# The diagonal of a gated scan: wide products by a matrix of ones, or sixteen one-column fp32 products

## The chip, the core and the metric

The kernel runs on one core of a Trainium2 chip. The metric is the device time of one execution in microseconds (us), as the median of several runs; the kernel before takes 483.58 us (three runs, 483.41 to 483.65). Engines are named as in the profile: PE is the matrix engine (TensorE), PEld its weight loads, DVE the vector engine, ACT the scalar engine, POOL GpSimd, SP the engine that issues most DMAs.

## What is computed

The reference is one decoder layer on 256 tokens of width 1024. A normalised input goes through one wide projection `w_in`. Its columns feed two branches: HGRN2, a gated linear recurrence with 8 heads of 128 channels, and block attention with 8 heads of 128. Both are projected, gated, summed, projected again, and a SwiGLU feed-forward part follows. All arrays are fp32.

The change touches the recurrence alone. Inside a chunk the reference computes

```
diff  = b[:, :, :, None, :] - b[:, :, None, :, :]
decay = exp(where(causal, diff, -inf))
attn  = einsum('bhtk,bhsk,bhtsk->bhts', q_, k_, decay)
```

where `b` is the running sum of the log gates. On the diagonal, t equals s, the decay is 1, and the entry is the plain sum over the 128 channels k of q times k at that token. That diagonal, for 2 blocks of 128 tokens and 8 heads, is what the changed code produces.

## The kernel before, in words

**Layout.** Tokens are handled in two blocks of 128. For the recurrence, `Q`, `K` and the gate `Fg` lie with channels on the partitions: [128 channels, 2 token blocks, 8 heads, 128 tokens]. The scores `A` of the recurrence lie as [128 tokens, 2 blocks, 8 heads, 128 tokens]. A routine `hgrn_diag` writes the diagonal (and zeros beside it) into all of `A`; then seven levels, `hgrn_level(0)` to `hgrn_level(6)`, lay the off-diagonal squares of doubling size over it with `COPY_PREDICATED` (L383). So `A` has to hold the diagonal before level 0 copies into it.

**Precision.** PE multiplies the big projections in the type fp32r. To keep fp32 precision each operand is cut in two halves, a high one (a cast on ACT, L55) and a low one (a subtraction on DVE, L56), and each product is made of three matmuls: high by high, high by low, low by high. Weights arrive by DMA as `wraw` and become `whi` and `wlo`; each of the three names has three buffers. `tok_block` (L83, L84, L85) is such a projection with 8 chunks of 128 rows by 512 columns for two token blocks: 48 matmuls, on two loads of weights of 4 chunks each. A matmul whose operands are plain fp32 needs no halves; the trace then shows two weight loads and two matmul records for one instruction.

**The diagonal before.** `hgrn_diag` multiplies Q by K into `qk` on DVE (L346), casts the high half `qkh` on ACT and subtracts the low half `qkl` on DVE (helper `split`, L55 and L56). `hgrn_diag_put` then runs, for two token blocks and two groups of four heads, two matmuls with a 128 x 128 matrix of ones as stationary operand and 512 columns of a half as moving operand (L356): each output row holds the sum over channels. DVE multiplies the result by the identity into `A` (L357), four times.

**Around it.** PE has just finished the two halves of the attention keys (`ktok`, columns 5120 and up). After the diagonal come level 0 (16 fp32 matmuls of 64 x 64, L377, on half the array's columns each), the first half of the attention queries (`qtok`, 48 wide matmuls), level 1, and the transposes of `ktok` (L422). Before those, `keys` normalises `ktok`: sums of squares on ACT (L413), scale and square root and reciprocal (L216, L217, L218), and two multiplications on DVE (L432).

**Order.** Up to the end of the attention a scheduler orders each engine's instructions when the program is built; each engine then runs its own list in order and waits on semaphores. PE takes the weights of the next matmul while one runs. From the middle stage on, the order is written out by hand and is the same in both kernels.

Of the kernel before, what the change touches and what calls it, by code (L numbers as in the profile page):

```python
# [7 lines left out]
F32 = mybir.dt.float32  # L8
F32R = mybir.dt.float32r
# [5 lines left out]
P = 128  # L15
# [3 lines left out]
H = 8  # L19
# [8 lines left out]
def tile_hgrn2_moba_block(ctx: ExitStack, tc: tile.TileContext, xm, xw, table, runs,  # L28
                          w_in, w_hg, w_at, w_out, w_gate, w_up, w_down, out):
    nc = tc.nc  # L30
    const = ctx.enter_context(tc.tile_pool(name="const", bufs=1))
    big = ctx.enter_context(tc.tile_pool(name="big", bufs=1))
    wp = ctx.enter_context(tc.tile_pool(name="wp", bufs=3))
    small = ctx.enter_context(tc.tile_pool(name="small", bufs=1))
# [9 lines left out]
    def pa(name="pa"):  # L44
        return psum.tile([P, 512], F32, name=name, tag="pa", bufs=2)
# [8 lines left out]
    def split(src, hi, lo):  # L54
        high = nc.scalar.copy(hi, src)  # L55
        return high, nc.vector.tensor_sub(lo, src, hi.bitcast(F32))  # L56
# [79 lines left out]
    for kt in range(KT):  # L136
        n0 = 0 if kt == 0 else NV
        t = big.tile([P, NX + D - n0], F32, name=f"xw{kt}", tag=("T3", "T4", "T5", "T1", "T7", "T8", "T9", "T11")[kt])
# [8 lines left out]
    ones = const.tile([P, P], F32, name="ones")  # L147
# [47 lines left out]
    ones_r = const.tile([P, P], F32R, name="ones_r")  # L195
    nc.gpsimd.tensor_copy(ones_r, ones)
    ident = const.tile([P, P], F32, name="ident")
# [6 lines left out]
    for j in range(7):  # L204
        c = 1 << j
        n = 64 // c
        for tb in range(2):
            m = mask[:, j, tb, :].rearrange("p (n c) -> p n c", c=c)
# [70 lines left out]
    for half in range(2):  # L279
        ps = F0 if half == 0 else feat_block(w_in, 1024 + half * 512, XT, cut=2 - half)  # L280
        for j in range(2):
            h = half * 4 + j * 2
# [44 lines left out]
    for half in range(2):  # L327
        ps = feat_block(w_in, half * 512, XT)
        for j in range(2):
            h = half * 4 + j * 2  # L330
# [7 lines left out]
    A = big.tile([P, 2, H, P], F32, name="A", tag="T5")  # L338
# [2 lines left out]

    def hgrn_diag():
        qk = big.tile([P, 2, H, P], F32, name="qk", tag="T9")
        qkh = big.tile([P, 2, H, P], F32R, name="qkh", tag="T10")
        qkl = big.tile([P, 2, H, P], F32R, name="qkl", tag="T8")
        nc.vector.tensor_mul(qk, Q, K)  # L346
        nc.vector.tensor_mul(QA, Q, Fg)
        split(qk, qkh, qkl)
        return qkh, qkl

    def hgrn_diag_put(qkh, qkl):
        for tb in range(2):
            for g in range(2):
                bank = (ph, pa)[g]().rearrange("p (h t) -> p h t", h=4)
                for m, part in enumerate((qkh, qkl)):
                    nc.tensor.matmul(bank, ones_r, part[:, tb, 4 * g:4 * g + 4, :], start=(m == 0), stop=(m == 1))  # L356
                nc.vector.tensor_mul(A[:, tb, 4 * g:4 * g + 4, :], bank,  # L357
                                     ident.unsqueeze(1).to_broadcast([P, 4, P]))

    def hgrn_level(j, small_bank=ph):  # L360
        Fc = decay[j]
# [46 lines left out]
    def qk_block(tok, sq, c0, half, bank=pw):  # L408
        put_tok(tok, tok_block(w_in, c0 + half * 512, XT, bank=bank), half)
        for tb in range(2):  # L410
            for h in range(half * 4, half * 4 + 4):
                jk = small.tile([P, P], F32, name="jk")
                nc.scalar.activation(jk, tok[:, tb, h * P:(h + 1) * P], AF.Square, accum_out=sq[:, tb, h:h + 1])  # L413
# [89 lines left out]
    kss = small.tile([P, 2, H], F32, name="kss")  # L503
    qk_block(ktok, kss, 5120, 0, bank=pa)
    qk_block(ktok, kss, 5120, 1)
    qkd = hgrn_diag()
    hgrn_diag_put(*qkd)
    hgrn_level(0)
    qtok = big.tile([P, 2, D], F32, name="qtok", tag="T8")
    qss = small.tile([P, 2, H], F32, name="qss")  # L510
# [704 lines left out]
```

## Time and profile before

| | before |
|---|---|
| median of 3 runs | 483.58 us |
| the profiled execution | 483.81 us |
| its span, first to last instruction | 482.1 us |
| granted PE clock, mean over the span | 1.000 |
| PE busy | 477.1 us (99%) |
| DVE busy | 405.8 us (84%) |
| ACT busy | 322.2 us (67%) |
| POOL busy | 37.3 us (8%) |

The 1.7 us between the profiled execution's time and its span lie before its first and after its last instruction. A row of the timeline gives the start, the length, the engine, the line, the operation, output and inputs, the number of merged instructions, and in brackets how long the engine sat idle before it and what ended that. Matmul records overlap, since the next one starts streaming while the last one drains: the cost of a matmul in a row of them is the distance from start to start, not its length. Starts and ends are given to 0.01 us.

### The profile page before, as it was taken

The numbers are of one execution on the slowest core, as the hardware profiler recorded it, in microseconds if no ns is written. First come the engines' busy times: TensorE is split into PE (matmuls) and PEld (weight loads), VectorE is DVE, ScalarE is ACT, GpSimd is POOL, SyncE is SP. The second block draws the span as 40 slices with busy tenths as digits, with TensorE's granted clock in tenths as the row PEclk, the third lists the DMA queues.
The fourth block names the chain that finished last, engine by engine and source line by source line (L and its number), as shares of the span: only waits on it lengthen the run. The fifth ranks groups of instructions, "written<-read, shape, count | busy, mean of one in ns | idle before, by whom it ended". The sixth has DMA issues, their size and how long they took to land.

```text
span 482.1 us, 6427 instructions
## 1 busy us (share of the span) xinstructions
PE 477.1 (99%) x2514; PEld 399.5 (83%) x2514; DVE 405.8 (84%) x402; ACT 322.2 (67%) x433; POOL 37.3 (8%) x73
## 2 busy tenths in 40 slices
PE   8999999999999999999999999999999999999997
PEld 7888888888888889887888888888888888888886
DVE  5878999698669987989999667899999999788863
ACT  5978645768756985789767645776786559747520
POOL 0930220000000000010000000000000000000000
PEclk9999999999999999999999999999999999999999
DMA  8978595634542345978896764799978979996502
GB/s 295 402 263 257 152 334 176 208 109 126 198 147 69 128 154 183 388 217 235 255 277 193 232 209 170 247 281 230 333 261 218 337 196 283 365 253 136 175 0 87
DMA packets 44125, 105.83 MB, mean 220 GB/s; under 512 B 1848, under 2 KB 4152, under 8 KB 42304
## 3 DMA queue, kind: packets, MB, share of 16 engines
q1 hardware_dynamic: 41344, 88.11, 52.6%
q0 software_dynamic: 2752, 17.33, 17.1%
q8 instruction: 19, 0.31, 0.3%
q14 instruction: 10, 0.08, 0.0%
HBM read 89.67 MB, written 1.07 MB: 188 GB/s over the span
## 4 chain that ended last, share of the span: by engine, by line
PE 92%; DVE 4%; ACT 2%; DMA 1%; issue 0%; SPq 0%; ACTq 0%
PE acc L1065 12%; PE late L571 12%; PE pw L814 10%; PE f L571 6%; PE pw L101 6%; PE pw L83 5%; PE pw L84 5%; PE pw L85 5%; PE pw L960 5%; PE pw L165 4%; PE pa L571 3%; DVE wlo L552 2%; PE pw L100 2%; PE pw L103 2%; DMA xw<-xw 1%; PE pw L959 1%
## 5 line engine op out<-in xcount | busy, mean ns | idle before, releaser
L548 ACT CAST whi<-W 128x2048 fp32r<-128x2048 f32 x42 | 79.9, 1912 | 42.4 <-DVE W L639 23.4
L552 DVE TENSOR_TENSOR wlo<-W,whi 128x2048 fp32r<-128x2048 f32 x42 | 95.6, 2288 | 10.6 <-ACT whi L548 9.9
L552 DVE TENSOR_TENSOR wlo<-wraw,whi 128x2048 fp32r<-128x2048 f32 x29 | 66.2, 2288 | 7.5 <-ACT whi L548 7.3
L548 ACT CAST whi<-wraw 128x2048 fp32r<-128x2048 f32 x29 | 55.5, 1918 | 14.3 <-PE pw L814 7.0
L56 DVE TENSOR_TENSOR wlo<-wraw,whi 128x2048 fp32r<-128x2048 f32 (+1 forms) x26 | 55.0, 2125 | 10.8 <-ACT whi L55 10.7
L55 ACT CAST whi<-wraw 128x2048 fp32r<-128x2048 f32 (+1 forms) x26 | 46.0, 1779 | 10.3 <-PE pw L85 5.6
L83 PE MATMUL pw<-whi,XT 128*128 128x512 f32 x112 | 44.2, 395 | 0.0
L85 PE MATMUL pw<-whi,XT 128*128 128x512 f32 x112 | 43.8, 391 | 0.0
L84 PE MATMUL pw<-wlo,XT 128*128 128x512 f32 x112 | 43.7, 390 | 0.0
L101 PE MATMUL pw<-XT,whi 128*128 128x512 f32 x128 | 40.6, 395 | 0.0
L645 POOL DMA_DIRECT2D W<-W x14 | 12.1, 862 | 345.4 <-ACT whi L548 161.9
L960 PE MATMUL pw<-x2T,whi 128*128 128x512 f32 x96 | 31.2, 396 | 0.0
L571 PE MATMUL late<-whi,C 128*128 128x512 f32 x96 | 30.4, 392 | 0.0
L1065 PE MATMUL acc<-whi,hq 128*128 128x512 f32 x92 | 29.4, 393 | 0.0
L83 PEld LDWEIGHTS pw<-whi,XT 128*128 128x128 f32 x112 | 21.0, 188 | 4.4
L85 PEld LDWEIGHTS pw<-whi,XT 128*128 128x128 f32 x112 | 21.0, 188 | 4.3
L84 PEld LDWEIGHTS pw<-wlo,XT 128*128 128x128 f32 x112 | 21.1, 188 | 4.2
L571 PE MATMUL late<-whi,x2T 128*128 128x512 f32 x72 | 23.3, 394 | 0.0
L639 DVE TENSOR_TENSOR W<-W,W 128x2048 f32<-128x2048 f32 x10 | 22.9, 2288 | 0.2
L571 PEld LDWEIGHTS late<-whi,C 128*128 128x128 f32 x96 | 18.0, 188 | 3.9 <-ACT q L663 0.2
L571 PE MATMUL f<-whi,C 128*128 128x512 f32 x64 | 20.8, 396 | 0.2 <-ACT q L663 0.2
L814 PE MATMUL pw<-whi,M 128*128 128x512 f32 x64 | 20.7, 396 | 0.0
(339 smaller groups left out, 1117.9 us busy)
## 6 DMA issues: line engine op xcount, KB each, us to landing
wraw<-w_in SPq DMA_DIRECT2D x22, 1024.0 KB, 5.1
W<-W POOLq DMA_DIRECT2D x14, 1024.0 KB, 8.6
wraw<-w_down SPq DMA_DIRECT2D x11, 1024.0 KB, 7.8
W<-w_in SPq DMA_DIRECT2D x8, 1024.0 KB, 7.4
W<-w_gate SPq DMA_DIRECT2D x8, 1024.0 KB, 7.3
W<-w_up SPq DMA_DIRECT2D x8, 1024.0 KB, 8.5
wraw<-w_at SPq DMA_DIRECT2D x4, 1024.0 KB, 6.5
wraw<-w_hg SPq DMA_DIRECT2D x4, 1024.0 KB, 7.2
```

Source lines behind the costliest of these rows:

```text
L55: high = nc.scalar.copy(hi, src)
L56: return high, nc.vector.tensor_sub(lo, src, hi.bitcast(F32))
L83: nc.tensor.matmul(ps[tb], part(act, kt, 0)[:, ts], wh, start=(kt == 0), stop=False)
L84: nc.tensor.matmul(ps[tb], part(act, kt, 0)[:, ts], wl, start=False, stop=False)
L85: nc.tensor.matmul(ps[tb], part(act, kt, 1)[:, ts], wh, start=False, stop=(kt == KT - 1))
L101: nc.tensor.matmul(ps[ct], hi[:, i, cs], both, start=(kt == 0), stop=(kt == KT - 1))
L548: nc.scalar.copy(t["hi"], raw())
L552: nc.vector.tensor_sub(t["lo"], raw(), t["hi"].bitcast(F32))
L571: nc.tensor.matmul(bank, act(kt, m), h[:, kt, :], start=(first and kt == 0 and m == 0 and h is hi), stop=(kt == 3 and m == 1), skip_group_ ...
L814: nc.tensor.matmul(blocks[key][tb], part(act, k0 + i, m)[:, tb * P:(tb + 1) * P], t[w][:, i, :], start=(k0 + i == 0 and m == 0 and w == "hi"),
L960: nc.tensor.matmul(block["ps", up][ct], t["hi"][:, i, cs], both, start=(kt == 0), stop=(kt == KT - 1))
L1065: nc.tensor.matmul(bank, ACTS[f0 + i](m, ts), w[:, i, c0:c0 + cw], start=(st and i == 0 and m == 0 and w is t["hi"]), stop=(en and i == 1 ...
```

## The change

The halves `qkh` and `qkl` go, and with them a cast on ACT and a subtraction on DVE. The eight wide matmuls go. In their place 16 fp32 matmuls, one for each block and head, take a 128 x 128 piece of `qk` as the stationary operand and one column of ones as the moving operand; each writes one column of 128 tokens into one bank of PSUM. ACT copies the 16 columns to SBUF (`dd`). DVE multiplies the identity by `dd`, both repeated by stride 0, into `A`: two instructions of 1024 columns in place of four of 512. `Q` times `K` and `Q` times `Fg` stay.

```diff
     def hgrn_diag():
         qk = big.tile([P, 2, H, P], F32, name="qk", tag="T9")
-        qkh = big.tile([P, 2, H, P], F32R, name="qkh", tag="T10")
-        qkl = big.tile([P, 2, H, P], F32R, name="qkl", tag="T8")
         nc.vector.tensor_mul(qk, Q, K)
         nc.vector.tensor_mul(QA, Q, Fg)
-        split(qk, qkh, qkl)
-        return qkh, qkl
-
-    def hgrn_diag_put(qkh, qkl):
+        return qk
+
+    def hgrn_diag_put(qk):
+        bank = pa("diag")
         for tb in range(2):
-            for g in range(2):
-                bank = (ph, pa)[g]().rearrange("p (h t) -> p h t", h=4)
-                for m, part in enumerate((qkh, qkl)):
-                    nc.tensor.matmul(bank, ones_r, part[:, tb, 4 * g:4 * g + 4, :], start=(m == 0), stop=(m == 1))
-                nc.vector.tensor_mul(A[:, tb, 4 * g:4 * g + 4, :], bank,
-                                     ident.unsqueeze(1).to_broadcast([P, 4, P]))
+            for h in range(H):
+                c = tb * H + h
+                nc.tensor.matmul(bank[:, c:c + 1], qk[:, tb, h, :], ones[:, 0:1], start=True, stop=True)
+        dd = small.tile([P, 2, H], F32, name="dd")
+        nc.scalar.copy(dd.rearrange("p b h -> p (b h)"), bank[:, 0:2 * H])
+        for tb in range(2):
+            nc.vector.tensor_mul(A[:, tb], ident.unsqueeze(1).to_broadcast([P, H, P]),
+                                 dd[:, tb, :].unsqueeze(2).to_broadcast([P, H, P]))
...
-    qkd = hgrn_diag()
-    hgrn_diag_put(*qkd)
+    hgrn_diag_put(hgrn_diag())
```

The scheduler also moves neighbours. On ACT, around the end of `ktok` and the normalisation of the keys (a row gives line, operation, output and inputs, shape, and how often it stands in a row; + is new, - is gone):

```order
 L259 ACTIVATE ktok<-pw,rx 128x512
 L413 ACTIVATE jk,kss<-ktok 128x128
+L355 COPY dd<-diag 128x16
 L55 CAST whi<-wraw 128x2048
 L413 ACTIVATE jk,kss<-ktok 128x128
 L365 COPY KP<-K 128x2x256x2
 L413 ACTIVATE jk,kss<-ktok 128x128 x5
+L55 CAST whi<-wraw 128x2048
 L217 ACT_TABLE_LOAD
 L217 ACTIVATE rk<-rk 128x16
-L55 CAST whi<-wraw 128x2048
```

The copy of `dd` stands ahead of a weight cast, the remaining sums of squares and the copy `KP`; the next weight cast moved ahead of the square root `rk`.

On DVE, before, from level 0's copies into `A` to level 1's (`rk` is the scale of the keys, `wlo` the low half of a weight chunk):

```order
L383 COPY_PREDICATED A<-mask,ph 64x8x32 x4
L394 TENSOR_TENSOR QA<-QA,Fg 128x2x512
L396 TENSOR_TENSOR K<-K,F_976 128x2x256x2
L216 TENSOR_SCALAR rk<-kss 128x16
L56 TENSOR_TENSOR wlo<-wraw,whi 128x2048
L218 RECIPROCAL rk<-rk 128x16
L432 TENSOR_TENSOR ktok<-ktok,rk 128x1024 x2
L56 TENSOR_TENSOR wlo<-wraw,whi 128x2048
L383 COPY_PREDICATED A<-mask,pa 64x8x16x2 x4
```

And in the changed kernel, from the new multiplications on:

```order
L357 TENSOR_TENSOR A<-ident,dd 128x1024 x2
L383 COPY_PREDICATED A<-mask,ph 64x8x32 x4
L394 TENSOR_TENSOR QA<-QA,Fg 128x2x512
L396 TENSOR_TENSOR K<-K,F_977 128x2x256x2
L216 TENSOR_SCALAR rk<-kss 128x16
L56 TENSOR_TENSOR wlo<-wraw,whi 128x2048 x2
L218 RECIPROCAL rk<-rk 128x16
L432 TENSOR_TENSOR ktok<-ktok,rk 128x1024 x2
L383 COPY_PREDICATED A<-mask,pa 64x8x16x2 x4
```

The second weight subtraction moved from behind the two multiplications of `ktok` to ahead of them.

On PE, the transposes of `ktok` behind level 1, before:

```order
L377 MATMUL pa<-QA,KP 64x2x32 x16
L422 MATMUL pa<-ident,ktok 128x128 x4
L422 MATMUL ph<-ident,ktok 128x128 x4
L422 MATMUL pw<-ident,ktok 128x128 x4
L422 MATMUL ph<-ident,ktok 128x128 x4
L83 MATMUL pw<-whi,XT_73 128x512
```

And in the changed kernel:

```order
L377 MATMUL pa<-QA,KP 64x2x32 x16
L422 MATMUL pa<-ident,ktok 128x128
L422 MATMUL ph<-ident,ktok 128x128
L422 MATMUL pw<-ident,ktok 128x128
L422 MATMUL ph<-ident,ktok 128x128
L83 MATMUL pw<-whi,XT_73 128x512
L84 MATMUL pw<-wlo,XT_73 128x512
L85 MATMUL pw<-whi,XT_73 128x512
L422 MATMUL pa<-ident,ktok 128x128 x3
L422 MATMUL ph<-ident,ktok 128x128 x3
L422 MATMUL pw<-ident,ktok 128x128 x3
L422 MATMUL ph<-ident,ktok 128x128 x3
```

The transposes are cut in two groups of 4 and 12, with three wide matmuls between them. Apart from a weight cast on ACT that moves ahead among the sums of squares behind level 1, nothing else changes places on PE, DVE and ACT, and the order of the DMA issues is the same.

## The prediction

> **What bounds the kernel now.** I read the page's first part, then the waits of PE, then PE's timeline around the diagonal.
>
> ```profile
> span 482.1 us, 6427 instructions
> PE 477.1 (99%) x2514; PEld 399.5 (83%) x2514; DVE 405.8 (84%) x402; ACT 322.2 (67%) x433; POOL 37.3 (8%) x73
> PE f L571 <- ACT q L663: 0.2, 1, 0.2
> PE f L571 <- DVE wlo L552: 0.2, 1, 0.2
> 97.60:482.00 384.40, 380.85 (x2010) 318.15 (x2008) 326.07 (x289) 254.25 (x328) 12.80 (x15) 1.00 0.68 209
> 478.66 0.28 PE L1065 MATMUL pw<-whi,hq 128*128 128x256 f32 x1
> ```
>
> The page gives PE 477.1 of 482.1 us. The two waits are the only ones of a whole PE, past the start, that the view of waits lists: 0.2 us each, in a later stage. The last row is a stretch of the windows view: from 97.6 us on, PE is busy 380.85 of 384.40 us; of the missing 3.55, 3.1 lie behind its last matmul (the last row, a line of the timeline), where the output drains. So nothing downstream waits for a spare engine: a microsecond that PE loses at the diagonal is a microsecond at the end, and one that it gains too, as far as the others keep up.
>
> ```profile
> 94.29 0.39 PE L85 MATMUL pw<-whi,XT 128*128 128x512 f32 x1
> 94.52 0.39 PE L356 MATMUL ph<-qkh,ones_r 128*128 128x512 f32 x1
> 94.75 0.39 PE L356 MATMUL ph<-qkl,ones_r 128*128 128x512 f32 x1
> 96.16 0.39 PE L356 MATMUL pa<-qkl,ones_r 128*128 128x512 f32 x1
> 96.48 1.16 PE L377 MATMUL ph<-QA,KP 128*64 128x64 f32 x32
> 97.56 0.50 PE L83 MATMUL pw<-whi,XT 128*128 128x512 f32 x1
> 97.90 0.39 PE L84 MATMUL pw<-wlo,XT 128*128 128x512 f32 x1
> 96.47 1.02 PEld L377 LDWEIGHTS ph<-QA,KP 128*64 128x64 f32 x32 [0.36 <-DVE A L357]
> ```
>
> The diagonal holds PE from 94.52 to 96.48, where level 0 starts: **1.96 us**, eight matmuls 0.23 apart and a last step of 0.32. The bracket names a wait for DVE before level 0. It is not one:
>
> ```profile
> 122.25 0.39 PE L85 MATMUL pw<-whi,XT 128*128 128x512 f32 x1
> 122.57 0.63 PE L377 MATMUL ph<-QA,KP 128*64 128x64 f32 x14
> ```
>
> Level 2 starts the same 0.32 behind a wide matmul that has nothing to do with DVE. A step from the whole array to 64 columns costs 0.32 - 0.23 = 0.09 more than a plain step, here as there. So no wait goes away with L357; what goes is eight matmuls.
>
> **The change on PE.** Sixteen fp32 matmuls, two records each as for every plain fp32 matmul (level 0 has 16 instructions and x32). The moving operand has one column, so the array streams next to nothing; what is left is loading 128 columns of weights 32 times. The trace has no stream like it, so I bound the price of a record.
>
> ```profile
> 97.56 0.19 PEld L83 LDWEIGHTS pw<-whi,XT 128*128 128x128 f32 x1
> 97.67 0.19 PEld L84 LDWEIGHTS pw<-wlo,XT 128*128 128x128 f32 x1
> 187.26 1.79 PE pw L703 x16
> L703 PEld LDWEIGHTS pw<-QA,K x16: 192/192/193, 187.0 to 188.7; 128*128 128x128 f32 x16
> L377 PEld LDWEIGHTS ph<-QA,KP x160: 132/138/139, 96.5 to 182.1; 128*64 128x64 f32 x160
> ```
>
> The first weight load after level 0 lies bare. Its matmul is logged 0.11 longer than its neighbours (0.50 against 0.39), and the next load starts 0.11 us after the first: a load of 128 columns takes 0.11, and the next can start only when the weights before it go into use. The lengths of the load records agree: 192 ns for 128 columns against 138 for 64, 54 ns for 64 columns. And eight fp32 products of K and QA, with 128 columns on both sides (L703, from the chain), take 1.79 for 16 records, **0.112 each**. There the moving operand would give the same price, so that row alone doesn't tell; the bare load does. I take 0.112: 31 steps between 32 records are 3.47, and the step out to level 0 loses the 0.21 that a wide matmul streams (0.32 - 0.21 = 0.11). Together **3.58 us, where 1.96 stood: +1.62**.
>
> From below, level 0 itself: its 32 records, alternating between the two halves of the array's columns, take 1.09 from 96.48 to 97.56, 0.034 each; by that the block is 31 x 0.034 + 0.11 = 1.16, or -0.80. From above, no overlap at all: a load of 0.11 and then 0.11 for the product to drain before the next load may start, 0.22, is 31 x 0.22 + 0.11 = 6.93, or +4.97. I stay with 0.112, since the 128-column bare load is the same operation on the same columns, while level 0 loads half as many and in two halves.
>
> The Trainium skill (page "TensorE: Matmul & The Clock Gate", section "Back-to-back issue gap") puts a matmul of 1 to 64 moving columns at about 60 cycles, 25 ns at full clock. By that figure, an estimate, 32 records would take 0.8 us and the change would gain about 1.1. The load in front of each isn't in that figure; the bare load of 0.11 speaks against it, and no stream of this trace has so few moving columns. Its side is the rival of cheap loads below, priced by rows.
>
> **The change on ACT and DVE.** Gone are the cast `qkh` and the subtraction `qkl`, both long done when PE needs them:
>
> ```profile
> 76.91 1.92 ACT L55 CAST qkh<-qk 128x2048 fp32r<-128x2048 f32 x1 [1.78 <-issue]
> 83.36 2.28 DVE L56 TENSOR_TENSOR qkl<-qk,qkh 128x2048 fp32r<-128x2048 f32 x1
> ```
>
> PE reads them at 94.5, eleven and nine microseconds after their starts, and no weight chunk in between is late for PE: worth nothing. What is added comes behind PE's block, and there the keys hang:
>
> ```profile
> 97.68 2.67 DVE L383 COPY_PREDICATED A<-mask,ph 64x256 f32<-64x256 uint32 x4
> 101.50 1.22 DVE L396 TENSOR_TENSOR K<-K,F 128x1024 f32<-128x1024 f32 x1
> 102.63 0.17 DVE L216 TENSOR_SCALAR rk<-kss 128x16 f32<-128x16 f32 x1
> 102.71 2.29 DVE L56 TENSOR_TENSOR wlo<-wraw,whi 128x2048 fp32r<-128x2048 f32 x1
> 104.91 0.25 DVE L218 RECIPROCAL rk<-rk 128x16 f32<-128x16 f32 x1
> 105.25 2.36 DVE L432 TENSOR_TENSOR ktok<-ktok,rk 128x1024 f32<-128x1024 f32 x2
> 103.34 1.92 ACT L55 CAST whi<-wraw 128x2048 fp32r<-128x2048 f32 x1 [0.29 <-PE pw L85]
> 102.83 0.22 ACT L217 ACTIVATE rk<-rk 128x16 f32<-128x16 f32 x1 [0.36 <-DVE rk L216]
> 109.76 0.66 PE L422 MATMUL pa<-ident,ktok 128*128 128x128 f32 x4
> 110.25 0.60 PE L422 MATMUL ph<-ident,ktok 128*128 128x128 f32 x4
> ```
>
> Before, the keys are ready at 107.6 and PE transposes them at 109.76: a slack of 2.1. After:
> - The last of the 32 records starts at 94.52 + 3.47 = 97.99, its result lands some 0.17 later (a length of 0.39 less 0.22 of streaming), ACT copies 16 columns (like L217, 0.22), DVE starts at about 98.45. Two instructions of 1024 columns, each 1.13 from start to start as L396 (101.50 to 102.63), end at about 100.75. Level 0's copies started at 97.68, so DVE is 3.07 late there.
> - From there to the first L432 it was 105.25 - 97.68 = 7.57. Now a second weight subtraction stands in between, 2.20 from start to start: 9.77. The first L432 starts at 100.75 + 9.77 = 110.52 and ends at 111.7.
> - The second subtraction needs a cast that waits for PE to finish a chunk (103.34 before, about 105.0 now) and ends near 106.9; the square root waits behind it and a table load until about 108.4; DVE gets there at 110.2. Neither decides.
> - PE arrives at the transposes at 109.76 + 1.62 = 111.38 and finds the first half of the keys at 111.75: **0.37 of stall**, new. The other 12 transposes need the second half, at 112.9; after 4 transposes (4 x 0.11) and three wide matmuls (0.69) PE asks for it at 112.9. That one just fits.
>
> Without the split of the transposes the stall would be longer; without the moved subtraction there would be none. Its bounds are 0 (DVE 0.4 quicker) and about 1.2 (the new multiplications, whose both inputs repeat by stride 0, a third slower than L432).
>
> Behind the transposes DVE catches up:
>
> ```profile
> 123.77 1.58 DVE L383 COPY_PREDICATED A<-mask,ph 64x256 f32<-64x256 uint32 x4 [2.29 <-PE ph L377]
> 137.51 1.13 DVE L451 SCALAR_TENSOR_TENSOR S<-pa,rq,B 128x128 f32<-128x128 f32 x4 [3.69 <-PE pa L447]
> ```
>
> DVE ends the second L432 at 112.9 where it did at 107.6, 5.3 later; 2.2 of that is the subtraction moved ahead, and PE itself is 2.0 later. The 1.1 of lag that is left is taken up where DVE idles for PE, 2.29 us before level 2's copies and 3.69 before the scores. The buffers: `diag` takes a PSUM bank that was freed at `ktok`'s copy; `qk` now lives until 98.1, but its place goes to `kT`, which is written after the transposes. Nothing more is moved.
>
> **The sum.** 483.81 (the profiled execution) + 1.62 + 0.37 = 485.80. The median before lies 0.23 below that execution, so **485.6 us**, +0.4%. The likeliest case's own range is 485.1 (no stall, 0.108 a record) to 486.6.
>
> **The rivals.**
> - *Cheap loads: not slower.* The two loads of an instruction, or those of neighbours, overlap as in level 0 and cost 0.034. For it: 32 records in 1.09 us there. Against it: the bare load, and 0.112 for L703. PE -0.80; the keys would be ready at 109.3 and PE there at 108.97, so the stall stays near 0.35: 483.1. The sum is zero at 0.048 a record, (1.96 - 0.11 - 0.35) / 31, and passes +0.2% at 0.08.
> - *No overlap: slower still.* With so short a stream a load can't hide, 0.22 a record: +4.97 and the stall, 488.9. For it: the 0.11 that the step to level 0 shows behind a stream's end. Against it: that step changes the shape of the array, and plain steps don't show it.
> - *The clock falls.* For 3.5 us the array computes almost nothing, and its clock may be taken back. What half clock costs stands at the start:
>
> ```profile
> 1.12 3.78 PE L153 MATMUL warm<-ones 128*128 128x128 f32 x16 [1.12 <-DVE ones L148]
> 4.88 1.35 PE L165 MATMUL pw<-whi,XT 128*128 128x512 f32 x3
> 6.07 0.62 PE L165 MATMUL pw<-wlo,XT 128*128 128x512 f32 x2
> ```
>
> 16 records in 3.76 us, 0.235 each against 0.112, and wide ones 0.40 apart until about 6; then 0.23. PE needed some 4.9 us of work to get its full clock. If that comes back behind the diagonal, half of it is lost: 2.45 more, 488.0. Against it: the windows view grants 1.00 in every later stretch; but none of them is as empty. The Trainium skill (page "TensorE: Matmul & The Clock Gate", section "What's actually happening") has the gate fall after one idle window of about 3.4 us, and doesn't say there whether weight loads count as work. No run so far shows it.
>
> **How the numbers follow.** Forecast 0.74; cheap loads 0.12; no overlap 0.06; the clock 0.06; 0.02 for a gain from elsewhere. A measurement of this kernel tells about 0.2% (1 us) from no change. The forecast, no overlap and the clock are slower by more: 0.85, taking off 0.01 for the forecast's low end. Cheap loads reach from 482.8 to 484: two thirds within 0.2%, a third faster. So faster 0.05, same 0.10, slower 0.85. The range: from 483.4, inside the cheap loads, to 487.0, above the forecast's own; some 0.06 are left out below and 0.12 above.
>
> **What would show it.** PE's 32 records 0.107 to 0.115 apart, from 94.5 to 98.0, and 0.10 to 0.12 from the last to level 0. Two L357 of about 1.2 us, from 98.4. PE waiting for L432 before the first transposes, 0.1 to 0.8. DVE idle again before level 2's copies, and no other new wait of PE. Wrong would be: a pitch under 0.05 or over 0.2, a granted clock under 1.00 near 100 us, or PE waiting for a weight half.

## The result and the profile after

| | before | changed |
|---|---|---|
| median | 483.49 us (6 runs, 483.07 to 483.65) | 486.62 us (6 runs, 486.05 to 489.46) |
| the profiled execution, its span | 483.81, 482.1 us | 486.29, 484.6 us |
| mean granted clock, span | 1.000 | 0.996 |

The ratio is 1.0072, with a 95% interval of 1.0058 to 1.0086: slower by 3.1 us. The page of the changed kernel gives PE still as the bound, 2.7 us busier, with one slice of its clock row below 9:

```profile
span 484.6 us, 6474 instructions
PE 479.8 (99%) x2538; PEld 402.7 (83%) x2538; DVE 403.3 (83%) x399; ACT 320.7 (66%) x433; POOL 37.1 (8%) x73
PEclk9999999989999999999999999999999999999999
```

PE's timeline around the diagonal in the changed kernel, from the last wide matmul ahead of it:

```profile
93.60 0.39 PE L85 MATMUL pw<-whi,XT 128*128 128x512 f32 x1
93.83 3.63 PE L353 MATMUL diag<-ones,qk 128*128 128x1 f32 x32
97.39 1.45 PE L377 MATMUL ph<-QA,KP 128*64 128x64 f32 x32
98.77 0.80 PE L83 MATMUL pw<-whi,XT 128*128 128x512 f32 x1
99.36 0.63 PE L84 MATMUL pw<-wlo,XT 128*128 128x512 f32 x1
99.79 0.63 PE L85 MATMUL pw<-whi,XT 128*128 128x512 f32 x1
...
101.49 0.40 PE L83 MATMUL pw<-whi,XT 128*128 128x512 f32 x1
101.73 0.40 PE L84 MATMUL pw<-wlo,XT 128*128 128x512 f32 x1
...
112.24 0.33 PE L422 MATMUL pa<-ident,ktok 128*128 128x128 f32 x1
```

The block runs from 93.83 to 97.39, 3.56 us for 32 records. Behind it the wide matmuls of the next projection stand 0.43 apart (99.36 to 99.79) where they stood 0.23 apart before; from 101.49 they are at 0.23 to 0.24 again. The windows view says why. Its rows give a stretch, its length, the busy time of PE, PEld, DVE, ACT and POOL with counts, then the granted clock, the DMA share and the GB/s. For the changed kernel, the block, the way from level 0 to the transposes, and three equal stretches around the place:

```profile
93.83:97.39 3.56, 3.56 (x34) 3.54 (x32) 0.00 (x0) 1.47 (x6) 0.00 (x0) 1.00 0.91 292
97.39:112.24 14.85, 14.85 (x113) 12.13 (x112) 13.93 (x14) 10.26 (x23) 0.00 (x0) 0.89 0.25 82
94.67:98.08 3.41, 3.41 (x47) 3.40 (x49) 0.38 (x1) 1.25 (x5) 0.00 (x0) 1.00 0.74 279
98.08:101.49 3.41, 3.41 (x22) 2.72 (x19) 3.40 (x5) 3.38 (x8) 0.00 (x0) 0.50 0.00 0
101.49:104.91 3.42, 3.42 (x16) 2.82 (x15) 3.41 (x5) 1.25 (x7) 0.00 (x0) 1.00 0.00 0
```

And for the kernel before, the block and the same way behind it:

```profile
94.52:96.48 1.96, 1.96 (x10) 1.32 (x8) 1.30 (x3) 1.93 (x7) 0.00 (x0) 1.00 0.81 210
96.48:109.76 13.28, 13.28 (x113) 10.97 (x113) 13.15 (x14) 9.61 (x22) 0.00 (x0) 1.00 0.36 127
```

Two terms come out. The block took 3.56 us where 1.96 stood: +1.60. The 113 matmul records from level 0 to the transposes took 14.85 us where 13.28 stood: +1.57, and in them lie 3.413 us at exactly half the clock, from 98.08 to 101.49. Half of 3.413 is 1.71; nearly all of it is lost. Together +3.17, against 3.13 between the medians. (The spans differ by 2.5 only because in this execution the block began 0.69 earlier, at 93.83 and not 94.52.)

The third term, PE's stall for the keys, isn't there. Past the start, PE's waits in the changed kernel are the two of before:

```profile
PE f L570 <- ACT q L662: 0.2, 1, 0.2
PE f L570 <- DVE wlo L551: 0.2, 1, 0.2
```

DVE's timeline shows that the keys are late, but PE is later still:

```profile
97.70 2.36 DVE L357 TENSOR_TENSOR A<-ident,dd 128x1024 f32<-128x1024 f32 x2 [4.79 <-ACT dd L355]
...
107.77 2.29 DVE L56 TENSOR_TENSOR wlo<-wraw,whi 128x2048 fp32r<-128x2048 f32 x1 [0.50 <-ACT whi L55]
...
110.31 2.36 DVE L432 TENSOR_TENSOR ktok<-ktok,rk 128x1024 f32<-128x1024 f32 x2
```

The first L432 ends at about 111.5 (half of 2.36 behind 110.31). PE comes to the transposes at 112.24; at full clock it would have come 13.28 behind 97.39, at 110.67. The half clock delays the keys as well: the subtraction at 107.77 waits 0.50 for a weight cast, and that cast could start only at 105.82, when PE had finished an earlier weight chunk (ACT waited 2.98 us for L85).

So the theory to test has two parts: 32 bare weight loads cost 1.6 whatever streams behind them, and a stretch in which PE loads and hardly streams takes half of its clock away for the 3.413 us behind it. The rivals: the half clock is chance, or comes from somewhere else in the program; and the price of a record is not the load's.

### The profile page after: what moved, and what is told of

It is laid out like the page before. It is cut to its first block, busy times and chain, and to the rows that moved or that the text cites. A ratio compares the mean times of both kernels' runs of the same rounds, so it can differ in the third digit from the quotient of the medians.

```text
span 484.6 us, 6474 instructions
## 1 busy us (share of the span) xinstructions
PE 479.8 (99%) x2538; PEld 402.7 (83%) x2538; DVE 403.3 (83%) x399; ACT 320.7 (66%) x433; POOL 37.1 (8%) x73
## 4 chain that ended last, share of the span: by engine, by line
PE 94%; DVE 4%; ACT 1%; issue 0%; ACTq 0%
PE acc L1064 12%; PE late L570 12%; PE pw L813 10%; PE f L570 6%; PE pw L101 6%; PE pw L83 6%; PE pw L84 5%; PE pw L85 5%; PE pw L165 5%; PE pw L959 5%; PE pa L570 3%; DVE wlo L551 2%; PE pw L100 2%; PE pw L103 2%; PE ph L377 1%; PE pw L958 1%
## 5 line engine op out<-in xcount | busy, mean ns | idle before, releaser
L83 PE MATMUL pw<-whi,XT 128*128 128x512 f32 x112 | 44.8, 400 | 0.0
L85 PE MATMUL pw<-whi,XT 128*128 128x512 f32 x112 | 44.2, 395 | 0.0
L84 PE MATMUL pw<-wlo,XT 128*128 128x512 f32 x112 | 44.1, 394 | 0.0
L83 PEld LDWEIGHTS pw<-whi,XT 128*128 128x128 f32 x112 | 21.4, 191 | 4.6
L85 PEld LDWEIGHTS pw<-whi,XT 128*128 128x128 f32 x112 | 21.3, 190 | 4.5
L84 PEld LDWEIGHTS pw<-wlo,XT 128*128 128x128 f32 x112 | 21.3, 190 | 4.3
```

Of the source, the lines that this page charges most:

```text
L83: nc.tensor.matmul(ps[tb], part(act, kt, 0)[:, ts], wh, start=(kt == 0), stop=False)
L84: nc.tensor.matmul(ps[tb], part(act, kt, 0)[:, ts], wl, start=False, stop=False)
L85: nc.tensor.matmul(ps[tb], part(act, kt, 1)[:, ts], wh, start=False, stop=(kt == KT - 1))
```

## Experiments

Each is the changed kernel with the edit shown; "..." marks lines left out. Ratios are against the kernel before in the same series. "Clock" is the mean granted clock of an execution. A clock of 0.999 needs no fall that matters: in the profile of the kernel with the order of before (further down) the clock halves only in the last 0.8 us of the span, behind PE's last matmul, and that alone makes its mean 0.999.

### Is the loss in two parts? The block cut in two

```diff
+    qkd = hgrn_diag()
+    diag0 = ph("diag0")
+    hgrn_diag_put(qkd, 0, diag0)
     qk_block(ktok, kss, 5120, 1)
-    hgrn_diag_put(hgrn_diag())
+    diag1 = pa("diag1")
+    hgrn_diag_put(qkd, 1, diag1)
+    hgrn_diag_end((diag0, diag1))
```

Each call of `hgrn_diag_put` makes the 8 products of one token block; between them lie 48 wide matmuls.

> The 16 one-column products in two groups of 8, the first between the two halves of the keys' projection, the second where all 16 stood. Theory: one block of 3.56 us leaves most of a 3.4 us window of the clock gate without streaming, so PE runs at half clock for the next window and loses 1.57; two blocks of 1.8 us don't. So: granted clock 1.000, two PE blocks of 1.8 us, time about 1.6 us (0.33%) over the kernel before, up to 2.0 if the keys stall PE by 0.37. Rival: the products cost their 3.1 us wherever they stand (the clock falls for them in any grouping): clock 0.996, 486.6 us.

Measured 486.24 us, ratio 1.0061 (1.0048 to 1.0074), and a clock of 0.999 or 1.000 in all five executions. The second group and level 0 behind it:

```profile
95.48 1.84 PE L350 MATMUL diag<-ones,qk 128*128 128x1 f32 x16
97.25 1.16 PE L377 MATMUL ph<-QA,KP 128*64 128x64 f32 x32
```

The same 32 records at the same price (these 16 take 1.77), and no half clock. The changed kernel had lost the clock in six executions of six, so this speaks against chance and against a source outside the block. But the time hardly fell, and lies above the 2.0 over the kernel before that was expected at most, because the stall that the half clock had covered now shows. PE's waits in this kernel:

```profile
PE pa L422 <- DVE ktok L432: 0.5, 1, 0.5
PE f L575 <- DVE wlo L556: 0.5, 1, 0.5
```

0.5 at the transposes, and in a later stage 0.5 for a weight half where 0.2 stood. So 1.6 + 0.5 + 0.3 = 2.4 of the 2.7 measured is named; the profiled execution itself took 485.77, 2.25 over the kernel before, and the slower ones left no trace. Why that later half came 0.3 later I did not find.

### Is it the load or the thin stream? 64 columns of ones

```diff
-        bank = pa("diag")
+        banks = [ph("diag0"), pa("diag1")]
...
-                c = tb * H + h
-                nc.tensor.matmul(bank[:, c:c + 1], qk[:, tb, h, :], ones[:, 0:1], start=True, stop=True)
+                c = 64 * h
+                nc.tensor.matmul(banks[tb][:, c:c + 64], qk[:, tb, h, :], ones[:, 0:64], start=True, stop=True)
...
-        nc.scalar.copy(dd.rearrange("p b h -> p (b h)"), bank[:, 0:2 * H])
+        for tb in range(2):
+            nc.scalar.copy(dd[:, tb, :], banks[tb].rearrange("p (h n) -> p h n", n=64)[:, 0:H, 0])
```

The 16 results now fill two banks, 8 to a bank, so `dd` takes two copies.

> The same 16 products in one block, but with 64 columns of ones as moving operand instead of one (the extra columns are not used). Theory: a record costs its bare weight load of 0.11, and 128 streamed rows (0.053) hide beneath it, so the block stays at 3.56 us; the array now streams half of the time, the clock stays at 1.000, and the time is 1.6 to 2.0 us over the kernel before. Rival: what counts for the clock is matmul work per load or the length of the block, not the streaming: the clock falls as in the changed kernel, 486.6 us. If streaming came on top of the load, the block would be 32 x 0.165 = 5.3 us.

Measured 485.33 us, ratio 1.0040 (1.0027 to 1.0052), clock 1.000 in all five. PE's timeline here, the block, level 0, and the transposes:

```profile
93.71 3.68 PE L353 MATMUL diag<-ones,qk 128*128 128x64 f32 x32
97.31 1.16 PE L378 MATMUL ph<-QA,KP 128*64 128x64 f32 x32
...
110.61 0.66 PE L423 MATMUL pa<-ident,ktok 128*128 128x128 f32 x4
```

and two stretches of 3.41 us of its windows view, the first of them with 3.15 us of the block in it:

```profile
94.16:97.57 3.41, 3.41 (x37) 3.34 (x38) 1.23 (x1) 2.99 (x8) 0.00 (x0) 1.00 0.83 294
97.57:100.98 3.41, 3.41 (x43) 2.92 (x38) 2.45 (x3) 2.74 (x12) 0.00 (x0) 1.00 0.00 0
```

64 times the columns, and the block takes 3.60 instead of 3.56: the load alone sets the price. From level 0 to the transposes it is 13.30, as before the change. So more streaming at the same length gives 1.55 us back there, all of it from the clock. Here the scheduler also put the second weight subtraction back behind the two multiplications of `ktok`, and there is no stall. What is left, +1.8, is the block's 1.64 and some 0.3 more at the late weight half of the first experiment, which is late here too.

### Where does it turn? 16 columns of ones

The same with `ones[:, 0:16]`; all 16 results then fit into the one bank of the changed kernel.

> As e2_n64, with 16 columns of ones as moving operand: 32 rows streamed per load, 0.013 of 0.111 us, a share of 12%, between that of one column (2%: the clock fell) and of 64 (48%: it stayed). Theory: the share of streaming in a window decides, with a threshold somewhere between; 12% is low, so the clock falls as in the changed kernel, 0.996 and 486.6 us. Rival: any sizeable stream counts, and the clock stays at 1.000: 485.3 us.

Measured 487.10 us, ratio 1.0076 (1.0061 to 1.0091), clock 0.993 to 0.996 in all four. The windows view of this kernel:

```profile
93.43:96.84 3.41, 3.41 (x31) 3.33 (x29) 0.00 (x0) 1.88 (x6) 0.00 (x0) 1.00 0.81 255
96.84:100.26 3.42, 3.42 (x39) 3.26 (x39) 2.09 (x2) 2.29 (x5) 0.00 (x0) 0.50 0.14 53
100.26:103.67 3.41, 3.41 (x9) 2.64 (x9) 3.38 (x6) 2.92 (x11) 0.00 (x0) 0.50 0.00 0
```

Here the half clock lasted two stretches of 3.413, the first of them still with the end of the block in it. How much of a record streams can be read from the shortest record of the group (lengths in ns, shortest, median, longest). With one column in the changed kernel:

```profile
L353 PE MATMUL diag<-ones,qk x32: 164/250/250, 93.8 to 97.2; 128*128 128x1 f32 x32
```

with 16 columns:

```profile
L353 PE MATMUL diag<-ones,qk x32: 177/263/375, 93.8 to 97.6; 128*128 128x16 f32 x32
```

and with 64:

```profile
L353 PE MATMUL diag<-ones,qk x32: 217/275/275, 93.7 to 97.1; 128*128 128x64 f32 x32
```

Sixteen columns add 13 ns to a record that comes every 112, 64 add 53: streaming for about 12% of the time loses the clock, for about 47% keeps it. Where between the two it turns was not tried.

### Loads on parts of the array: 64 and 32 weight columns

```diff
-                nc.tensor.matmul(bank[:, c:c + 1], qk[:, tb, h, :], ones[:, 0:1], start=True, stop=True)
+                for q in range(P // 64):
+                    qs = slice(64 * q, 64 * q + 64)
+                    nc.tensor.matmul(bank[qs, c:c + 1], qk[:, tb, h, qs], ones[:, 0:1], start=True, stop=True)
```

and the same with 32 in place of 64.

> Each product in two, of 64 weight columns on either half of the array's columns, as level 0 does it: 64 records. Theory: loads of 64 columns take 0.053, those of the two halves overlap as in level 0 (0.029 a record), so the block takes 1.9 us, like the eight wide matmuls: within 0.2% of the kernel before, clock 1.000. Rival: without streaming between them the loads go one by one, 64 x 0.056 = 3.6 us, and the clock falls: 486.6 us.

> Each product in four, of 32 weight columns on a quarter of the array's columns each: 128 records. If loads of four quarters overlap, a quartet takes about 0.04 us and the block 1.3 us: 0.7 us (0.14%) below the kernel before, or 0.2 below with the keys' stall. Rival: a record can't be issued faster than some 0.025 us: 128 of them take 3.2 us, 1.3 us above the kernel before, and then the clock falls as well, 2.8 above.

Measured 483.59 us with 64, ratio 1.0007 (0.9998 to 1.0016), and 484.93 with 32, ratio 1.0034 (1.0022 to 1.0047). The blocks in PE's timelines, with level 0 behind them, first 64 columns:

```profile
93.74 2.03 PE L355 MATMUL diag<-ones,qk 128*64 128x1 f32 x64
95.63 1.14 PE L379 MATMUL ph<-QA,KP 128*64 128x64 f32 x32
109.44 0.30 PE L424 MATMUL pa<-ident,ktok 128*128 128x128 f32 x1 [0.48 <-DVE ktok L434]
```

then 32:

```profile
94.28 1.24 PE L355 MATMUL diag<-ones,qk 128*32 128x1 f32 x128
95.46 1.28 PE L379 MATMUL ph<-QA,KP 128*64 128x64 f32 x32
110.22 0.30 PE L424 MATMUL pa<-ident,ktok 128*128 128x128 f32 x1 [1.26 <-DVE ktok L434]
```

The same weights in 64 records take 1.89 us, in 128 records 1.18; one by one, at 0.112 for 128 columns, either would take 3.6. So loads on different columns of the array overlap, and 0.112 is the price of a load of the whole array. The rival's floor of 0.025 a record is out as well: the quarters come every 0.009.

The clock is 0.999 or 1.000 in all but one of the sixteen executions. That one, with 64 columns, has 0.996 and took 484.54 us, the longest of the eleven: a stretch of half clock can come behind this block too. It left no trace.

And the keys' stall is there: 0.48 with 64 columns. With 32 it is 1.26 and again 0.98, because the scheduler put a weight cast ahead of the copy of `dd` and the multiplication of `QA` ahead of `A`, and cut the two multiplications of `ktok` apart. So the time with 32 columns missed the expectation: at 1.4 over the kernel before it is near the rival's 1.3, but for another reason, since the block took 1.18 and not 3.2.

### The cheap block with the order of before

The 32-column kernel, with edges that hold ACT and DVE to the order of the kernel before: the copy of `dd` ahead of the weight cast, the copies into `A` ahead of the multiplication of `QA`, and the second subtraction behind both multiplications of `ktok`.

```diff
+            with ExitStack() as held:
+                if after is not None:
+                    held.enter_context(tc.issue_after(after.ins))
+                nc.vector.tensor_mul(qv, qv, view(Fc, 0, [[fb + 1, 2], [2, H * n], [0, c]]))
...
+    hgrn_level(0, after=put)
...
+    behind.extend([(copied,), (root_k, scaled)])
```

`put` is the last multiplication into `A`; `behind` lists what the next weight casts have to come behind.

> The 32-column quarters of e4_col32 (block of 1.18 us), with the kernel before's order around them by edges to the scheduler: on ACT the copy of dd ahead of the next weight cast and the square root rk ahead of the one after, on DVE the multiplications by dd ahead of level 0's update of QA, and those of ktok ahead of the second weight subtraction. Theory: the 2.2 us that PE waited at the transposes in e4_col32 come from that order alone, so they go, and the time is 0.78 us (0.16%) below the kernel before: 482.7 us. Rival: the keys are late because DVE can only start on A after the diagonal; then PE still waits there, by 0.4 us or more, and the time is that of the kernel before or above.

Measured 482.62 us against 483.35, ratio 0.9988 (0.9980 to 0.9997): 0.7 us below the kernel before, as expected, and just clear of no change. PE's timeline:

```profile
93.62 1.25 PE L363 MATMUL diag<-ones,qk 128*32 128x1 f32 x128
94.79 1.18 PE L388 MATMUL ph<-QA,KP 128*64 128x64 f32 x32
108.11 0.66 PE L436 MATMUL pa<-ident,ktok 128*128 128x128 f32 x4
```

The block takes 1.17 (1.96 before, -0.79), level 0 to the transposes 13.32, and no wait stands between. DVE in this kernel:

```profile
104.97 2.36 DVE L446 TENSOR_TENSOR ktok<-ktok,rk 128x1024 f32<-128x1024 f32 x2
```

Both halves of the keys are done at 107.33, 0.8 ahead of PE: the stall of the 32-column kernel was the order alone.

### Can the loads hide under wide matmuls? One product behind every three

```diff
+                if between is not None:
+                    between(2 * kt + tb)
...
-    qk_block(ktok, kss, 5120, 1)
-    hgrn_diag_put(hgrn_diag())
+    qkd = hgrn_diag()
+    diag = ph("diag")
+
+    def one(c):
+        nc.tensor.matmul(diag[:, c:c + 1], qkd[:, c // H, c % H, :], ones[:, 0:1], start=True, stop=True)
+
+    qk_block(ktok, kss, 5120, 1, between=one)
+    hgrn_diag_end(diag)
```

`between` is called behind each group of L83, L84 and L85.

> The 16 one-column products one by one, each behind three wide matmuls of the second half of the keys' projection (columns 5120 and up). Theory: a load can hide only beneath the matmul just before it, so of an instruction's two loads and the wide matmul's load behind them two lie bare: 0.22 us an instruction, 3.56 in all, as in one block; the clock stays at 1.000; 1.6 us over the kernel before and what the keys wait, 485.1 to 486.2 us. Rival: PE takes loads from further ahead, they hide beneath the wide matmuls, and the 1.96 us of the kernel before's block go: 481.6 to 482.6 us.

Measured 487.34 us, ratio 1.0088 (1.0075 to 1.0101), clock 1.000 in all five. I had expected 485.1 to 486.2. One round of PE's timeline:

```profile
94.50 0.28 PE L506 MATMUL diag<-ones,qk 128*128 128x1 f32 x2
94.64 0.48 PE L83 MATMUL pw<-whi,XT 128*128 128x512 f32 x1
94.95 0.40 PE L84 MATMUL pw<-wlo,XT 128*128 128x512 f32 x1
...
95.41 0.28 PE L506 MATMUL diag<-ones,qk 128*128 128x1 f32 x2
```

A round takes 0.91, of which three wide matmuls are 0.68: a product costs 0.23, no less than in the block. The first of its two loads hides under L85, but the second lies bare (94.50 to 94.64), and the load for L83 behind it lies bare too (L83 to L84 is 0.31, not 0.23). From the first product at 83.48 to level 0 at 97.47 it is 13.99, less 45 wide matmuls at 0.227 (10.2): the sixteen cost 3.8, +1.8 against the block before. The rest stands in PE's waits:

```profile
PE pa L419 <- DVE ktok L429: 2.2, 2, 1.2
```

The two multiplications of `ktok` were cut apart here too, and the one of `QA` stands ahead of `A`. Together 4.0, the measured difference: the products cost what the theory gave, the keys' wait is what it missed.

### The block eleven microseconds earlier, and the grid

```diff
+    hgrn_diag_put(hgrn_diag())
     qk_block(ktok, kss, 5120, 1)
-    hgrn_diag_put(hgrn_diag())
```

The results go to a bank of `ph` here.

> The changed kernel's block of 16 one-column products as it is, but between the two halves of the keys' projection, with wide matmuls on both sides and 11 us ahead of level 0. Theory: the block alone is empty enough to take the clock for one window wherever it stands: clock 0.996, 1.6 + 1.6 + up to 0.2 for two changes of shape less: 486.5 us, without a wait at the transposes. Rival: the thin matmuls of level 0 behind the block are needed for it, and the clock stays at 1.000: 485.1 us.

Measured 486.40 us, ratio 1.0064 (1.0047 to 1.0080); but its executions differ. Four have a clock of 0.995 or 0.996 and took 486.39 to 488.14 us; two have 1.000 and took 485.12 and 485.44. Here the half clock came and went with the same program. In the traces so far, every change of the clock inside the program lay a whole multiple of 3.413 us behind the moment at which it first became whole (in the changed kernel 5.92, then 98.08, which is 27 windows later), and that moment differed by execution, from 4.7 to 6.8 us. (The record of the clock starts there, so a view prints 1.00 for the time before it, too.) So the place at which this grid cuts the block might decide. Three more profiled executions of the same kernel (one of the kernel before beside them took 484.10 us):

> The kernel of the early block once more, for one profiled execution, because its executions differed: four showed a mean clock of 0.995 or 0.996 and took 486.4 to 488.1 us, two showed 1.000 and took 485.1 and 485.4. The theory of a fixed grid: the clock is judged in windows of 3.413 us that are counted from the moment the clock is first whole (every stretch of whole clock in the traces so far was a whole number of them long, 24, 27, 112 and 116), so what decides is where the grid cuts the block of 3.49 us. Expected: half clock from the next grid line if one window holds more than some 2.3 us of the block, none if the line cuts it nearer its middle; 2.79 us fell in the profiled execution so far, and pieces of 1.77 never did. The rival: the clock answers to something outside the program; then falls and no falls show no relation to where the grid lies.

> The same kernel a second time, for another place of the grid. The same expectation: half clock if one window of 3.413 us holds more than some 2.3 us of the block, else none; the rival expects no relation.

> The same kernel a third time. The same expectation: half clock if one window of 3.413 us holds more than some 2.3 us of the block, else none; the rival expects no relation.

In the table the share is the longest part of the block that one window of the grid holds.

| execution | time | block | window | of the block in it | half clock after it | block to transposes |
|---|---|---|---|---|---|---|
| second | 485.56 | 83.44 to 86.92 | 85.07 to 88.48 | 1.86 us | none | 27.88 us |
| third | 486.14 | 82.54 to 86.03 | 83.72 to 87.13 | 2.31 us | one window | 29.47 us |
| first | 488.14 | 83.17 to 86.66 | 83.87 to 87.28 | 2.79 us | one window | 29.47 us |
| fourth | 488.41 | 83.14 to 87.03 | 82.77 to 86.18 | 3.04 us | two windows | 31.05 us |

The windows view of the fourth execution, on its grid:

```profile
82.77:86.18 3.41, 3.41 (x32) 3.33 (x30) 1.29 (x2) 1.89 (x6) 0.00 (x0) 1.00 1.03 393
86.18:89.59 3.41, 3.41 (x12) 2.93 (x12) 2.18 (x2) 2.35 (x5) 0.00 (x0) 0.50 0.50 185
89.59:93.01 3.42, 3.42 (x9) 2.65 (x9) 2.39 (x2) 1.94 (x10) 0.00 (x0) 0.50 0.00 0
```

and of the second:

```profile
85.07:88.48 3.41, 3.41 (x25) 3.14 (x26) 1.18 (x2) 1.38 (x2) 0.00 (x0) 1.00 0.93 351
```

The order by share is the order by half clock, as the grid theory had it (the third execution lay right at the 2.3 that I had given); a source outside the program would show such an order only by luck, though four executions are few. A window with 1.86 us of bare loads in its 3.41 kept the clock, one with 2.31 lost it, and each lost window costs 1.59 us on the way from the block to the transposes (27.88, 29.47, 31.05).

The times of whole executions don't show this as cleanly. The block itself begins up to 0.9 us earlier or later, and the first execution has a wait that the others have not: at 342.43 PE has waited 0.95 for ACT, which had waited 1.32 for a transfer of `W`, far behind the block.

Why the fourth execution lost a second window is open. Its first window held the largest share, 3.04 us, and its second one began with the end of the block, 0.85 us; the kernel with 16 columns, which also lost two, had both as well (its block runs from 93.84 to 97.86, so 3.00 and 1.02). In the profile of the changed kernel the window from 94.67 to 98.08 held 2.72 us of the block and 0.69 of level 0. The mean clock says how often that happens: half a window of 484.6 us is 0.0035, so by this count its five executions at 0.996 lost one window, and the one at 0.993 (489.46 us) two. That one is 2.9 us longer than the others, of which a second window explains 1.6; the rest has no trace.

The Trainium skill (page "TensorE: Matmul & The Clock Gate", section "What's actually happening") gives the window as 3413 ns, free-running, and knows only half and full rate. The traces agree with all three. What it says of an idle window is too narrow for this case: PE was busy for the whole 3.41 us here, and 0.69 of it, level 0, even streamed.

## Why the prediction was right, and where it was not

- **The bound.** Right. Every microsecond of PE came out at the end: 1.60 + 1.57 = 3.17 at PE, 3.13 in the medians.
- **A record costs 0.112.** Right: 3.56 for 32 records and the step to level 0, against 3.58. The choice of the bare 128-column load over level 0's 0.034 was the right one, and for the reason given: level 0 loads half as many columns, on alternating halves. The 64-column kernel, at 1.89 / 64 = 0.03 a record, comes to level 0's price by loading as level 0 does.
- **DVE's work gone is worth nothing.** No run tested it by itself, and none speaks against it.
- **The keys' stall of 0.37.** Not seen in the changed kernel, where PE came 1.57 later than the step assumed. Where the clock stays whole and the second subtraction stands ahead of L432, it is there: 0.48 with 64 weight columns and 0.5 with the block cut in two. The chain (`dd`, L357, level 0's copies, the moved subtraction, L432) was the right one at full clock: with 64 weight columns, whose block is 1.69 shorter than the 3.58 of the forecast, L432 starts 14.33 behind the block's start, against 16.00 - 1.69 = 14.31. In the changed kernel it is 110.31 - 93.83 = 16.48, 0.48 more, and that is the second subtraction's wait of 0.50 for its cast, of which the prediction had said that it doesn't decide. The half clock had held the cast up: it starts 11.99 behind the block's start, and 8.73 with 64 weight columns, whose measured block is 1.67 shorter, which leaves 1.59.
- **Cheap loads, no overlap.** Both wrong, by the pitch of 0.112.
- **The clock falls.** This was a rival at 0.06, and it is what happened. The step that failed is "Against it: the windows view grants 1.00 in every later stretch". Those stretches all stream, so they could not speak for one that doesn't; that was said, and then weighed too lightly. By the prediction's own list, a granted clock under 1.00 near 100 us meant that it was wrong, and the clock was 0.50 from 98.08 to 101.49. Its price was taken as 2.45, half of the 4.9 us at the start. It is one window of 3.413, and 1.57 to 1.59 of it lost.
- **The sum.** 485.6 from 1.62 + 0.37; what stands there is 1.60 + 1.57 + 0. The forecast is 1.0 us low, with the time inside its range: by the terms it is 1.57 - 0.37 - 0.02 = 1.18 low. That it still lay inside the range, 0.4 below its top, owes something to luck: half of the loss came from a rival that was priced at 488.0, outside the range. It cost less than that, and it hid the stall.

## What to carry to other kernels

A plain fp32 matmul loads its weights twice, and behind a thin moving operand those loads are the whole price: 0.22 us an instruction here for 128 columns, however few columns move and also between wide matmuls. Loading parts of the array in turn makes them cheap (64 columns 0.03 a record, 32 columns 0.009). Count a block in which PE mostly loads for some 2 us or more as a risk to the clock (one execution of eleven lost it with a block of 1.89), look for wide matmuls 0.43 apart behind it, and look at the order on the engines behind a block that was made shorter: the gain of the 32-column block showed only once the copies behind it were put first again.

## What the runs showed of the hardware

- Busy loading is not busy for the clock. Windows of 3.41 us in which PE's rows were 100% busy, but 2.3 us or more of them bare loads, brought half clock in every profile that has one; 64 moving columns behind the same loads did not, 16 did.
- The clock is judged on a grid of 3.413 us that the program doesn't set, so executions of one program differ by whole windows: none, one and two at half clock in the profiles of the early block, with 27.88, 29.47 and 31.05 us from the block to the transposes.
- A second window was lost in the two traces where the first one at half clock began with the end of the block still running (the fourth execution of the early block, and 16 columns). These two also had the largest share of the block in the window before, so the condition is not separated.
- Loads on different columns of the array overlap: 128 columns for 16 fp32 products took 3.56 us whole, 1.89 in halves, 1.18 in quarters.
